# Stores of the second half of w_out's operands: from SyncE's queue to GpSimd's

## The chip, the cores and the metric

The kernel runs on one core of a Trainium2 chip. The metric is the device time of one execution in microseconds (us). The core has five engines that run their own instruction streams and meet at semaphores: TensorE (PE), VectorE (DVE), ScalarE (ACT), GpSimd (POOL) and SyncE (SP). SP computes nothing here: it issues DMAs. ACT and POOL can issue DMAs too. Each of the three has its own instruction stream, in which a DMA that has to wait holds back whatever stands behind it.

## The reference

One layer of a streaming encoder over 4096 prompt rows and 32 sample rows of width 1024, all in float32:

```
h = rmsnorm(x);  proj = h @ w_in                    # 1024 x 5120
u, v, z_a, xb, z_b = split(proj)
a = u * chunk_mlp(layernorm(v)) * silu(z_a)         # mixing of positions, 8 heads
b = pool_mix(x_ext) * silu(z_b)                     # trailing means 2, 4, 8, 16, linear map by group
y = x + concat(a, b) @ w_out                        # w_out: 2048 x 1024
y_out = rmsnorm(y)
```

## The kernel before

Every large product is one step of a seven-product scheme on 2x2 blocks: each operand is turned into seven combinations (q = 0 to 6), each combination is split into a high part (rounded to TensorE's float32r) and a low part (the rest), and TensorE multiplies high by high, high by low and low by high. The program goes through these stages:

- a first stage makes v and the combinations of x, which are stored in DRAM (`xops`);
- four stages (`Set`), one per quarter of the rows, make a and b and store them transposed in DRAM (`abT`);
- two stages (`OutPair`, z = 0 and z = 1) multiply by the upper and the lower 1024 rows of w_out. The stage z = 0 adds its products to x and stores the sum in DRAM (`part`); z = 1 loads it, adds its own products, normalises and stores the output.

In an out stage the operands of w_out lie in seven big tiles (`slot`), one for each q, and pairs of 128 rows of a or b go by. A pair has seven steps (q = 0 to 6) of 12 matmuls. A step's matmuls end in a PSUM bank, and DVE adds the bank to the tile `y` (L724). ACT makes the high part of a pair's operand (L677), DVE the low part (L81), five steps ahead of the multiplication.

The operands of w_out are made beside the stage before the one that uses them and go through DRAM (`wops`). The object `OutWeights(z, k)` does it in seven steps for each of four k: ACT casts the high part (L119), DVE subtracts it to get the low part (L81), then the two, which lie side by side in one tile of 512 KB, are stored (L652). For z = 0 that tile is a `wop`; for z = 1 it is one of the six tiles `raw`. The 28 steps of z = 1 run beside the pairs of stage z = 0, one in every three of their steps. The six `raw` tiles also take the loads of the pairs' rows (L669, from `abT`), rows of w_in (L1209) and the sources of later steps. A tile that was stored from can be written again only when its store has landed. In stage z = 1, each `slot` is loaded from `wops` (L634) when PE has used up its old contents.

SP's stream holds, in this stretch, the loads of w_out (L646), of `abT` (L669), of x into `y` (L703), of w_in (L1209), of a small stack (L1207), and the 28 stores of the operands (L652). A load L703 into a `y` tile waits until the store of its old contents (L735, `part<-y`, in POOL's stream) has landed. There are six `y` tiles, two for each pair. A scheduler sets the order within each engine's stream from the order in the code and its own estimates.

Of the kernel before, what the change touches and what calls it, by code (L numbers as in the profile page):

```python
# [8 lines left out]
F32 = mybir.dt.float32  # L9
# [27 lines left out]
def stream_step(ctx: ExitStack, tc, x_prompt, x_sample, state_pool, norm_g, w_in, ln_v_g, ln_v_b,  # L37
# [9 lines left out]
    nc = tc.nc  # L47
# [63 lines left out]
    def weight_ops(a1, a2, b1, b2, sums, dst, in_order=False):  # L111


        keep = {}
        less = lambda o, x, y: nc.vector.tensor_tensor(o, x, y, ALU.subtract)  # L115

        def split(q, src):
            hi, lo, *then = dst(q)
            pair = nc.scalar.copy(hi, src), lo_part(lo, src, hi)  # L119
            if q == 0 and in_order:  # L120
                for ins in pair:
                    tc.keep_in_program_order(ins)
            if behind:
                behind.pop()
                tc.keep_in_program_order(pair[0])
            for step in then:
                step()

        def third():
            keep[1], keep[2] = sums(), sums()  # L130
            less(keep[1], b1, a1)
            less(keep[2], b2, keep[1])
            split(2, keep[2])

        def fourth():
            less(b1, b2, b1)
            split(3, b1)

        def last():
            less(a2, a2, keep[2])  # L140
            split(6, a2)

        return [lambda: split(0, a1), lambda: split(1, a2), third, fourth, lambda: split(4, keep[1]),
                lambda: split(5, b2), last]
# [66 lines left out]
    with ExitStack() as ph:  # L211
# [142 lines left out]
        class Past:  # L354


            def load(self):
                self.st = half(), half()
                for z in range(2):
                    nc.gpsimd.memset(self.st[z][:HALO], 0.0)  # L360
                    nc.sync.dma_start(self.st[z][1:HALO], state_pool[0, 0, :, z * 512:(z + 1) * 512])
# [259 lines left out]
    def raw_tile(dt=F32):  # L621
        return raw_p.tile([P, D], dt, tag="raw", name="raw")

    def weight_tile():
        return op_p.tile([P, 2, 4, P], F32R, tag="wop", name="wop")
# [10 lines left out]
    class OutWeights:  # L636
# [5 lines left out]
        def load(self):  # L642
            v = []
            for i in range(2):
                raw = self.tile()
                nc.sync.dma_start(raw, w_out_v[8 * self.z + 4 * i + self.k])  # L646
                v.append(raw.rearrange("p (s c e) -> p s c e", s=2, e=P))

            def dst(q):
                t = weight_tile() if self.z == 0 else raw_tile(F32R).rearrange("p (h k t) -> p h k t", h=2, k=4)  # L650
                out = wops[self.z, q, :, self.k, :]
                store = lambda: nc.sync.dma_start(out, t.rearrange("p h k t -> p (h k t)").bitcast(F32))  # L652
                return t[:, 0], t[:, 1], store

            self.prep = weight_ops(v[0][:, 0], v[1][:, 0], v[0][:, 1], v[1][:, 1], sum_tile, dst)
# [530 lines left out]
    with ExitStack() as ph:  # L1186
# [56 lines left out]
        for n in range(n_sets, len(groups)):  # L1243
# [6 lines left out]
            for m, (s, q) in enumerate(order):  # L1250
# [4 lines left out]
                k = n - n_sets - 4  # L1255
# [48 lines left out]
```

## Time and profile before

| | |
|---|---|
| time, median of 3 runs | 2347.77 us (2347.44 to 2348.26) |
| time of the profiled execution | 2347.65 us |
| its span | 2345.9 us |
| PE busy | 2328.8 us (99%) |
| DVE busy | 1790.2 us (76%) |
| ACT busy | 896.4 us (38%) |
| POOL busy | 215.1 us (9%) |
| TensorE clock granted | full, 0.999 over the span |
| share of DMA engines in q1 (SP's transfers and others of that kind) | 45.9% |
| share in q0 (transfers that POOL issues) | 8.3% |

The time is 1.75 us more than the span (2347.65 against 2345.9); what lies around the span isn't in the profile. The span is measured from the first to the last instruction. A wait in the profile names the engine and line that ended it; idle time matters only on the engine that sets the end.

### The profile page before, as it was taken

Reading aid. Unit: us, or ns where it says so; the run is one execution under the profiler, and the core shown is the slowest. Engines: PE = TensorE matmul, PEld = TensorE weight load, DVE = VectorE, ACT = ScalarE, POOL = GpSimd, SP = SyncE. Lnnn points to the kernel's source line nnn. Section 1 sums busy time; section 2 is a strip of 40 time slices with the busy share of each in tenths; the row PEclk is TensorE's granted clock in tenths of the full one; section 3 lists DMA queues with packets and bytes.
Section 4 is the critical chain, followed back from the end, with each engine's and each line's share of the span. In section 5 each row is a group of like instructions: output and inputs, shape, how many; then the busy total and the mean of one; then the engine's idle time right before and its main releaser. Section 6 shows DMA issues by size and latency. Waiting matters only on the chain.

```text
span 2345.9 us, 32604 instructions
## 1 busy us (share of the span) xinstructions
PE 2328.8 (99%) x11936; PEld 1981.3 (84%) x11936; DVE 1790.2 (76%) x3318; ACT 896.4 (38%) x1603; POOL 215.1 (9%) x398
## 2 busy tenths in 40 slices
PE   8999999999999999999999999999999999999998
PEld 7878888888888888888888899999987878888877
DVE  7877786866787767877668876668777778688887
ACT  6545544433433333433334333334322333233333
POOL 1010000100021000111000110102200000000000
PEclk9999999999999999999999999999999999999999
DMA  8879977432448334483334472335587776955542
GB/s 309 316 241 279 275 255 245 142 104 89 149 144 296 99 100 134 135 300 122 108 108 148 177 262 87 101 100 164 223 294 265 252 257 232 360 171 169 159 137 90
DMA packets 325145, 445.69 MB, mean 190 GB/s; under 512 B 19324, under 2 KB 248444, under 8 KB 322296
## 3 DMA queue, kind: packets, MB, share of 16 engines
q1 hardware_dynamic: 273384, 355.05, 45.9%
q0 software_dynamic: 22288, 73.48, 8.3%
q10 hardware_dynamic: 29312, 15.08, 2.4%
q8 instruction: 94, 1.54, 0.3%
q14 instruction: 67, 0.55, 0.1%
HBM read 273.88 MB, written 169.66 MB: 189 GB/s over the span
## 4 chain that ended last, share of the span: by engine, by line
PE 95%; DMA 2%; DVE 2%; issue 0%; ACT 0%; SPq 0%; ACTq 0%; DVEq 0%
PE acc L193 66%; PE acc L712 8%; PE acc L713 8%; PE acc L714 8%; PE sp L998 2%; PE tr L473 1%; DMA wops<-raw 1%; DMA vt<-in_w_in_dram 1%; PE acc L261 0%; DMA op<-in_w_in_dram 0%; PE more L844 0%; PE more L843 0%; DVE wop L81 0%; DVE y L724 0%; PE acc L202 0%
## 5 line engine op out<-in xcount | busy, mean ns | idle before, releaser
L193 PE MATMUL acc<-slot,wop 128*128 128x512 f32 (+1 forms) x6720 | 1260.9, 348 | 1.0 <-DVE wop L81 1.0
L193 PEld LDWEIGHTS acc<-slot,wop 128*128 128x128 f32 x6720 | 1081.1, 188 | 156.5 <-DVE wop L81 1.4
L81 DVE TENSOR_TENSOR wop<-raw,wop 128x512 fp32r<-128x512 f32 (+1 forms) x510 | 353.4, 695 | 133.0 <-ACT wop L119 121.7
L119 ACT CAST wop<-raw 128x512 fp32r<-128x512 f32 x340 | 210.5, 622 | 384.4 <-PE acc L193 266.9
L712 PE MATMUL acc<-slot,wop 128*128 128x512 f32 x892 | 347.2, 389 | 1.5 <-DVE y L724 1.5
L713 PE MATMUL acc<-slot,wop 128*128 128x512 f32 x892 | 347.1, 389 | 0.0
L714 PE MATMUL acc<-slot,wop 128*128 128x512 f32 x892 | 347.0, 389 | 0.0
L193 PE MATMUL acc<-slot,op 128*128 128x512 f32 x1344 | 323.8, 395 | 0.3 <-ACT vt L167 0.2
L193 PEld LDWEIGHTS acc<-slot,op 128*128 128x128 f32 x1344 | 247.6, 188 | 51.9 <-ACT vt L167 0.7
L165 DVE TENSOR_TENSOR t<-acc,t 128x512 f32<-128x512 f32 (+1 forms) x320 | 186.7, 584 | 120.0 <-ACT t L174 65.5
L724 DVE TENSOR_TENSOR y<-acc,y 128x512 f32<-128x512 f32 x235 | 159.3, 687 | 72.6 <-PE acc L714 72.2
L712 PEld LDWEIGHTS acc<-slot,wop 128*128 128x128 f32 x892 | 167.4, 188 | 37.8 <-ACT wop L677 2.3
L714 PEld LDWEIGHTS acc<-slot,wop 128*128 128x128 f32 x892 | 167.4, 188 | 34.8
L713 PEld LDWEIGHTS acc<-slot,wop 128*128 128x128 f32 x892 | 167.4, 188 | 34.7
L677 ACT CAST wop<-raw 128x512 fp32r<-128x512 f32 x160 | 98.7, 622 | 175.2 <-PE acc L714 164.9
L81 DVE TENSOR_TENSOR wop<-sum,wop 128x512 fp32r<-128x512 f32 x200 | 136.9, 685 | 25.7 <-ACT wop L119 24.9
L1017 POOL DMA_DIRECT2D abT<-t x128 | 69.2, 541 | 843.2 <-DVE t L1029 622.7
L119 ACT CAST wop<-sum 128x512 fp32r<-128x512 f32 x136 | 84.5, 622 | 96.9 <-PE acc L193 72.0
L1040 DVE TENSOR_TENSOR t<-t 128x527 f32<-128x527 f32 (+3 forms) x160 | 111.1, 698 | 0.6
L677 ACT CAST wop<-sum 128x512 fp32r<-128x512 f32 x64 | 39.7, 622 | 119.5 <-PE acc L714 96.3
L174 ACT COPY t<-acc 128x512 f32<-128x512 f32 (+1 forms) x80 | 40.2, 504 | 107.1 <-PE acc L193 105.4
L115 DVE TENSOR_TENSOR sum<-raw 128x512 f32<-128x512 f32 x68 | 46.8, 688 | 44.7 <-DMA raw<-in_w_in_dram 44.1
(236 smaller groups left out, 1955.0 us busy)
## 6 DMA issues: line engine op xcount, KB each, us to landing
raw<-in_w_in_dram SPq DMA_DIRECT2D x102, 512.0 KB, 4.3
xops<-op SPq DMA_DIRECT2D x72, 512.0 KB, 6.1
abT<-t POOLq DMA_DIRECT2D x128, 256.0 KB, 3.8
raw<-abT SPq DMA_DIRECT2D x64, 512.0 KB, 5.0
slot<-xops SPq DMA_DIRECT2D x30, 1024.0 KB, 9.6
slot<-wops SPq DMA_DIRECT2D x14, 2048.0 KB, 9.7
xt<-in_x_prompt_dram SPq DMA_DIRECT2D x32, 512.0 KB, 5.0
raw<-v_all SPq DMA_DIRECT2D x32, 512.0 KB, 3.3
```

What stands on the lines that cost most here:

```text
L81: return nc.vector.tensor_tensor(out, src, hi.bitcast(F32), ALU.subtract)
L119: pair = nc.scalar.copy(hi, src), lo_part(lo, src, hi)
L165: add = lambda o, x, y: nc.vector.tensor_tensor(o, x, y, ALU.add)
L193: mm(acc, stationary(s, k), moving(m, k), start=fresh and n == 0, stop=n == len(terms) - 1, skip_group_check=True)
L677: nc.scalar.copy(t[:, 0], src)
L712: mm(acc, x[:, 0, k, :], w[:, k, 0, c], start=fresh and k == 0, stop=False, skip_group_check=True)
L713: mm(acc, x[:, 0, k, :], w[:, k, 1, c], start=False, stop=False, skip_group_check=True)
L714: mm(acc, x[:, 1, k, :], w[:, k, 0, c], start=False, stop=k == 3, skip_group_check=True)
L724: nc.vector.tensor_tensor(y, self.acc[bank], y, ALU.add)
L998: mm(sp[:, a, :], self.v[:, 4 * hf + a, :], WT[:, h, :], start=True, stop=True)
L1017: nc.gpsimd.dma_start(abT[row, :, t0:t0 + HALF], t[:, :HALF])
L1040: tt(nxt[:, lo:HALO + m], s[:, lo:HALO + m], s[:, lo - step:HALO + m - step], ALU.add)
```

## The change

The store of an operand of w_out is issued by GpSimd when z is 1, and by SyncE, as it was, when z is 0. Tiles, sources, destinations and arithmetic stay the same.

```diff
             def dst(q):
                 t = weight_tile() if self.z == 0 else raw_tile(F32R).rearrange("p (h k t) -> p h k t", h=2, k=4)
                 out = wops[self.z, q, :, self.k, :]
-                store = lambda: nc.sync.dma_start(out, t.rearrange("p h k t -> p (h k t)").bitcast(F32))
+                queue = nc.gpsimd if self.z else nc.sync
+                store = lambda: queue.dma_start(out, t.rearrange("p h k t -> p (h k t)").bitcast(F32))
                 return t[:, 0], t[:, 1], store
```

One line is added, so line numbers above 652 rise by one: the store is L653 after the change, the load of `y` L704, the store of `part` L736.

The 28 stores leave SP's stream and enter POOL's. PE's stream keeps its order, and on DVE and ACT a few neighbours change places. In SP's stream of before, in the stretch from about 1900 to 1932 us, three stores of the operands (`raw_17286`, `raw_17347`, `raw_17414`) stand between loads:

```order
L669 DMA raw_17279<-abT_66 128x4x256
L669 DMA raw_17281<-abT_66 128x4x256
L703 DMA y_17521<-in_x_prompt_dram 128x1024
L703 DMA y_17522<-in_x_prompt_dram 128x1024
L652 DMA wops_70<-raw_17286 128x1024
L1209 DMA raw_17378<-in_w_in_dram 128x1024
L646 DMA spare_17277<-in_w_out_dram 128x1024
L652 DMA wops_70<-raw_17347 128x1024
L1207 DMA st_17376<-stk_74 128x128
L652 DMA wops_70<-raw_17414 128x1024
L669 DMA raw_17437<-abT_66 128x4x256
L703 DMA y_17690<-in_x_prompt_dram 128x1024
```

In SP's stream of the changed kernel, at the same place:

```order
L670 DMA raw_17279<-abT_66 128x4x256
L670 DMA raw_17281<-abT_66 128x4x256
L704 DMA y_17521<-in_x_prompt_dram 128x1024
L704 DMA y_17522<-in_x_prompt_dram 128x1024
L1210 DMA raw_17378<-in_w_in_dram 128x1024
L646 DMA spare_17277<-in_w_out_dram 128x1024
L1208 DMA st_17376<-stk_74 128x128
L670 DMA raw_17437<-abT_66 128x4x256
L670 DMA raw_17439<-abT_66 128x4x256
L704 DMA y_17690<-in_x_prompt_dram 128x1024
```

The stores are gone, and the second load from `abT` (`raw_17439`) now stands ahead of the load of `y_17690`. POOL's stream of before holds only the stores of `part` there:

```order
L735 DMA part_71<-y_17048 128x1024
L735 DMA part_71<-y_17049 128x1024
L735 DMA part_71<-y_17206 128x1024
L735 DMA part_71<-y_17207 128x1024
L735 DMA part_71<-y_17368 128x1024
```

POOL's stream of the changed kernel, at the same place:

```order
L736 DMA part_71<-y_17048 128x1024
L736 DMA part_71<-y_17049 128x1024
L653 DMA wops_70<-raw_17286 128x1024
L653 DMA wops_70<-raw_17347 128x1024
L653 DMA wops_70<-raw_17414 128x1024
L736 DMA part_71<-y_17206 128x1024
L736 DMA part_71<-y_17207 128x1024
L653 DMA wops_70<-raw_17483 128x1024
```

The three stores stand behind the stores of one pair's `part` and ahead of the next pair's.

## Rows read from the trace of the kernel before

**Rows 1.** The page: busy time of each engine, and the chain that ended last
```profile
PE 2328.8 (99%) x11936; PEld 1981.3 (84%) x11936; DVE 1790.2 (76%) x3318; ACT 896.4 (38%) x1603; POOL 215.1 (9%) x398
PE 95%; DMA 2%; DVE 2%; issue 0%; ACT 0%; SPq 0%; ACTq 0%; DVEq 0%
```

**Rows 2.** All waits of PE: line, releaser, us in total, times, longest
```profile
PE tr L402 <- DMA vt<-in_w_in_dram: 1.9, 1, 1.9
PE acc L712 <- DVE y L724: 1.5, 2, 1.1
```

**Rows 3.** PE's timeline round its two waits: start, us, engine, line, instruction
```profile
1871.97 0.39 PE L714 MATMUL acc<-slot,wop 128*128 128x512 f32 x1
1872.72 0.47 PE L712 MATMUL acc<-slot,wop 128*128 128x512 f32 x1 [0.37 <-DVE y L724]
...
1932.52 0.39 PE L714 MATMUL acc<-slot,wop 128*128 128x512 f32 x1
1934.05 0.47 PE L712 MATMUL acc<-slot,wop 128*128 128x512 f32 x1 [1.15 <-DVE y L724]
```

**Rows 4.** The chain of waits, 1845 to 1875 us: start, us, what
```profile
1851.04 0.68 DVE raw L81
...
1852.41 6.61 DMA wops<-raw
...
1859.78 0.70 DVE raw L81
1860.50 0.33 SPq L646
...
1860.87 5.45 DMA wops<-raw
```

**Rows 5.** The chain of waits, 1910 to 1936 us
```profile
1913.68 0.32 SPq L703
...
1914.09 6.23 DMA wops<-raw
...
1921.08 0.70 DVE raw L81
...
1922.17 5.47 DMA wops<-raw
```

**Rows 6.** DVE's timeline at 1911 us: the low part of the second chain's first tile
```profile
1911.58 0.68 DVE L81 TENSOR_TENSOR raw<-spare,raw 128x512 fp32r<-128x512 f32 x1
```

**Rows 7.** SP's waits, then ACT's, in 1740 to 2000 us
```profile
SPq L703 <- DMA part<-y: 73.7, 19, 11.5
...
ACT raw L119 <- DMA wops<-raw: 32.6, 9, 6.4
```

**Rows 8.** The stores on SP (L652), 1740 to 2000 us: count, ns, landing
```profile
L652 SPq DMA_DIRECT2D wops<-raw x28: 319/324/1298, 1745.5 to 1991.4; - x28
...
DMA to landing us min/median/max: 2.6/3.9/9.2
```

**Rows 9.** The stores of part on POOL (L735), 1700 to 2000 us
```profile
L735 POOL DMA_DIRECT2D part<-y x24: 531/531/557, 1759.8 to 1990.5; - x24
...
DMA to landing us min/median/max: 2.8/5.0/6.8
```

**Rows 10.** POOL's timeline at 1865 us: a store of part
```profile
1865.09 0.53 POOL L735 DMA_DIRECT2D part<-y  x1 [17.51 <-DVE y L724]
```

**Rows 11.** SP's timeline: loads of y and third store, then the slots
```profile
1867.80 0.32 SPq L652 DMA_DIRECT2D wops<-raw  x1
...
1991.44 0.32 SPq L652 DMA_DIRECT2D wops<-raw  x1
...
1996.06 5.77 SPq L634 DMA_DIRECT2D slot<-wops  x2
...
2006.94 19.36 SPq L634 DMA_DIRECT2D slot<-wops  x5
```

**Rows 12.** Busy time: us, PE, PEld, DVE, ACT, POOL, clock, DMA, GB/s
```profile
1740.00:2000.00 260.00, 258.48 (x1138) 209.98 (x1138) 194.49 (x303) 80.86 (x131) 14.97 (x28) 1.00 0.76 256
```

## The prediction

> **What bounds the kernel now.** I read the page first: PE is busy for 2328.8 of 2345.9 us and carries 95% of the chain that ended last [rows 1]. No queue can win more than the 17.1 us that PE isn't busy. Next, all of PE's waits over the whole span [rows 2]: the reader is to see that in the stage the change touches PE waits only twice, 1.5 us in all, for DVE's addition of a bank to `y`. The longest other wait, 1.9 us, is for a load ahead of the first products, which no moved store reaches; the rest are 1.4 us or less, all in earlier stages. So the ceiling of this change is small and can be read exactly. In this stage a matmul takes PE 258.48 / 1138 = 0.23 us [rows 12]; round the two waits the starts are once 0.75 us apart (1871.97 to 1872.72) and once 1.53 (1932.52 to 1934.05) [rows 3]. That is 0.52 + 1.30 = 1.82 us lost, a little more than the idle 0.37 + 1.15 that the view names, since the pipeline also has to fill again.
>
> Then I ask what made DVE late, in the chain of waits behind each of them [rows 4, 5]. The reader is to see the same pattern twice: a store `wops<-raw` of 6.2 to 6.6 us, then ACT's cast into that tile and DVE's subtraction, then a second store of 5.5 us. ACT's cast of the next operand waits until the store ahead of it has landed (32.6 us in 9 waits in this stretch, the longest 6.4 [rows 7]). ACT works in order, so the pairs' own casts (L677) and DVE's work behind them stand still too. PE lives on its lead of five steps and runs dry at the end of the second landing.
>
> **The change part by part.** *The issue of a store.* In the first chain the low part is ready at 1851.04 + 0.68 = 1851.72 and SP issues at 1852.41: 0.69 late. The second store is ready at 1859.78 + 0.70 = 1860.48 and goes out at 1860.87, behind the load L646: 0.39 late [rows 4]. In the second chain the first store is ready at 1911.58 + 0.68 = 1912.26 [rows 6] and goes out at 1914.09: 1.83 late, right behind a load of `y` (L703, 1913.68). The second is ready at 1921.08 + 0.70 = 1921.78 and goes at 1922.17: 0.39 late [rows 5]. SP stood at L703 because the old `y` had not yet landed in `part`; over the stretch that cost SP 73.7 us in 19 waits, the longest 11.5 [rows 7]. On POOL neither load stands ahead: the POOL order shows three stores in a row between two pairs' `part`. I take 0.05 us of lateness for each, as SP shows when nothing stands ahead (1860.48 to 1860.50, for the load L646). That removes 0.69 + 0.39 - 0.10 = 0.98 us from the first chain and 1.83 + 0.39 - 0.10 = 2.12 from the second.
>
> *The landing.* On SP the 28 stores land 2.6 to 9.2 us after issue, median 3.9 [rows 8]; the four in the chains took 6.61, 5.45, 6.23 and 5.47, since each goes out right behind another load. The trace shows no `wops` store on POOL. The nearest row is POOL's store of `part`, the same 512 KB from SBUF to DRAM in the same stretch: 2.8 to 6.8 us, median 5.0 [rows 9]. I take 5.0, and keep 2.8 and 6.8 as ends.
>
> *How much the chain may take.* A chain's length is its two latenesses and two landings. The first is 0.69 + 6.61 + 0.39 + 5.45 = 13.14 us and PE loses 0.52, so PE loses nothing at 12.62. The second is 1.83 + 6.23 + 0.39 + 5.47 = 13.92 and loses 1.30: again 12.62. That both give the same number is why I trust it. On POOL: 0.10 + 5.0 + 5.0 = 10.1 us, 2.5 below the limit, so both waits go. With the landings exactly as they were on SP the chains are 0.10 + 12.06 = 12.16 and 0.10 + 11.70 = 11.80, and both waits still go, by 0.46 and 0.82. With 6.8 each it is 13.7, PE loses 1.08 twice, 2.16 instead of 1.82: 0.3 slower than before. With 2.8 the waits just go.
>
> *What POOL pays.* 28 issues of 0.531 us [rows 9] are 14.9 us more on an engine that is busy 14.97 of 260 [rows 12]. The price is order: a store of `part` that now stands behind the third store of a chain is late. In the first chain it was issued at 1865.09 [rows 10]; the third `wops` store went out at 1867.80 [rows 11]; so `part` goes at 1868.3, 3.2 us late. Waiting for it is SP's load of x into that `y`, which is for the third pair after (six tiles, two a pair; a pair is 7 steps of 12 matmuls at 0.23, some 19 us). Two pairs of cover hide 3.2 us; without cover it would be 3.2 us of PE in each of the two places.
>
> *What SP gains and loses.* 28 issues of 0.32 us go [rows 8], hidden anyway. Loads issue earlier where a store was ahead of them. The second load from `abT` now stands ahead of two loads of `y`; it waits for the landing of the chain's third store, as it did. Its reader comes several steps later, and the `y` behind it have the cover above. I cost both at nothing.
>
> *The change of stage.* The last store was issued at 1991.44 and the seven slots are loaded from 1996.06 on [rows 11], each when PE lets go of the old one. On POOL that store stands behind `part` of a finished pair and the small store L1239. A few us late would still meet slots of which the last are loaded some 30 us later. Nothing is taken for it.
>
> *A rule that speaks against it.* POOL's issue of `part` takes 531 to 557 ns [rows 9] while DVE is busy 194.49 of 260 us [rows 12], so the row shows no issue held up by a DVE instruction. The Trainium skill's page "SBUF — State Buffer" (Summary: rules for kernel authors) advises against a GpSimd DMA under DVE work: its descriptors are written by GpSimd, which a DVE instruction in one of the faster modes locks out, so one should issue from ACT or SP. By the rule this would cost what the last rival below costs; by the rows, nothing.
>
> **The sum.** 2347.65 (own time of the profiled execution) - 1.82 = 2345.83. The median of the runs shown is 2347.77, 0.12 above it, so the median should come to 2345.95; I say 2346.0.
>
> **The rivals.**
> - *The landing eats it.* POOL's stores share the DMA engines (0.76 busy in this stretch [rows 12]) with the same loads, and land in 6.4 to 6.8 us. For it: 6.8 has been seen on POOL. Against: the median of 5.0. The waits stay as they were or half: 2346.7 to 2348.1, about 2347.7.
> - *Slower: a store on POOL lands in 9.2 us*, as the longest on SP did [rows 8], because loads that SP no longer holds back all run beside it. Place: the cast L119 in the same two chains. The chain is then 0.10 + 18.4 = 18.5, PE loses 18.5 - 12.62 = 5.9 twice, 11.8 instead of 1.82: 2357.7. It decides from landings of 6.26 us on the mean (half of 12.52), and makes the kernel slower than before from 6.7. Against: no POOL store of 512 KB in the stretch was above 6.8.
> - *POOL's issue held by DVE.* If each store waits for one DVE subtraction of 0.68 us [rows 6], the first chain is 12.16 + 1.36 = 13.52 and loses 0.90, the second 11.80 + 1.36 = 13.16 and loses 0.54; 1.44 instead of 1.82: 2347.4 on the scale of the median.
>
> **How the numbers follow.** Both waits go: 0.66. The landing eats it: 0.21. Held by DVE: 0.05. Slower: 0.08, of which more than half is less than the full price. A measurement of this kernel can tell 0.2%, 4.7 us, from no change. The first three cases lie within it. Faster by more would need PE time that no row shows: 0.01. Slower by more is the worst part of the slower case: 0.03. So 0.96 for no change. The range: below, 2345.95 less the spread of the runs shown (0.4) is 2345.5, taken as 2345.3; above, 2348.4, which takes in the case of landings of 6.8 and the spread, and leaves out most of the slower case.
>
> **What would show it.** Right: in the changed kernel PE has no wait on L724's additions in the out stages, the matmuls follow 0.23 us apart all through, ACT's waits for `wops<-raw` fall below 32.6 us, POOL's L653 lands at about 5 us, and SP still stands at L704 but nothing of PE hangs on it. Wrong: waits of PE on L724 of over 1.5 us, L653 landing above 6.7 us, or PE waiting for a `y` or `abT` load that was not late before.

## The result and the profile after

The changed kernel took 2354.54 us, median of 9 runs (2353.38 to 2358.07); the kernel before took 2348.05 beside it (9 runs, 2346.07 to 2349.99). The ratio is 1.0029, 95% interval [1.0021, 1.0038]: slower by 6.5 us, more than the 0.2% that the prediction took as the least change that can be told. The prediction of 2346.0 us with a range up to 2348.4 and 0.03 for slower was wrong. The profiled execution took 2353.82 us with a span of 2352.0, 6.1 more than before.

The page after, to be set against [rows 1]:

```profile
PE 2332.2 (99%) x11936; PEld 1984.0 (84%) x11936; DVE 1789.9 (76%) x3318; ACT 895.6 (38%) x1603; POOL 230.3 (10%) x426
PE 92%; issue 3%; DMA 2%; DVE 2%; ACT 0%; POOL 0%; SPq 0%; POOLq 0%; DVEq 0%; ACTq 0%
```

PE is still 99% busy. It does the same 11936 matmuls, yet its busy time rose by 3.4 us: some matmuls ran slower. PE's two largest items of waiting over the span (line, releaser, us in total, times, longest), against [rows 2]:

```profile
PE acc L713 <- DVE y L725: 6.0, 3, 3.8
PE tr L402 <- DMA vt<-in_w_in_dram: 1.6, 2, 0.9
```

The two waits of 1.5 us for the addition into `y` became three of 6.0 us. PE's timeline shows where (start, us, engine, line, instruction, idle before it):

```profile
1792.05 0.39 PE L715 MATMUL acc<-slot,wop 128*128 128x512 f32 x1
1793.72 0.47 PE L713 MATMUL acc<-slot,wop 128*128 128x512 f32 x1 [1.28 <-DVE y L725]
...
1799.06 0.39 PE L715 MATMUL acc<-slot,wop 128*128 128x512 f32 x1
1803.22 0.76 PE L713 MATMUL acc<-slot,wop 128*128 128x512 f32 x1 [3.77 <-DVE y L725]
1803.78 0.63 PE L714 MATMUL acc<-slot,wop 128*128 128x512 f32 x1
1804.20 0.63 PE L715 MATMUL acc<-slot,wop 128*128 128x512 f32 x1
...
1808.47 0.56 PE L713 MATMUL acc<-slot,wop 128*128 128x512 f32 x1
1808.87 0.39 PE L714 MATMUL acc<-slot,wop 128*128 128x512 f32 x1
...
1879.21 0.39 PE L715 MATMUL acc<-slot,wop 128*128 128x512 f32 x1
1880.51 0.47 PE L713 MATMUL acc<-slot,wop 128*128 128x512 f32 x1 [0.91 <-DVE y L725]
```

Less the pace of 0.23, the start-to-start gaps cost 1.44, 3.93 and 1.07 us. Behind the second, 13 matmuls take 5.65 us (1803.22 to 1808.87) instead of 13 x 0.23 = 2.99, another 2.66. That is 9.1 us, against 1.82 before: 7.3 more. The stage starts about 1.0 us earlier than before (the first slot load at 1671.63 instead of 1672.63), which leaves 6.3, beside 6.1 in the spans. The wait that stood at 1933 before is gone; the one near 1872 has a counterpart at 1879. The big one, near 1799, and the one at 1792 have no counterpart in [rows 2].

What released it is on DVE and ACT. DVE's timeline of the changed kernel, then ACT's:

```profile
1795.41 0.69 DVE L692 TENSOR_TENSOR raw<-raw,sum 128x512 f32<-128x512 f32 x1
1801.78 0.69 DVE L81 TENSOR_TENSOR raw<-spare,raw 128x512 fp32r<-128x512 f32 x1 [5.67 <-ACT raw L119]
1802.39 0.68 DVE L725 TENSOR_TENSOR y<-acc,y 128x512 f32<-128x512 f32 x1
1802.99 0.68 DVE L81 TENSOR_TENSOR wop<-sum,wop 128x512 fp32r<-128x512 f32 x1
```
```profile
1792.16 1.13 ACT L678 CAST wop<-raw 128x512 fp32r<-128x512 f32 x2
1801.13 0.62 ACT L119 CAST raw<-spare 128x512 fp32r<-128x512 f32 x1 [7.83 <-issue]
1801.65 0.61 ACT L678 CAST wop<-sum 128x512 fp32r<-128x512 f32 x1
```

DVE stands still for 5.67 us at the subtraction of an operand of w_out, and the addition that empties PE's bank stands right behind it. The subtraction waits for ACT's cast, and the cast (which the view gives as "issue") starts 0.07 us after the seventh store has landed: that store is issued at 1793.27 and lands at 1801.06. The same place on DVE in the kernel before:

```profile
1796.18 0.69 DVE L724 TENSOR_TENSOR y<-acc,y 128x512 f32<-128x512 f32 x1 [0.65 <-PE acc L714]
1796.83 0.69 DVE L81 TENSOR_TENSOR wop<-sum,wop 128x512 fp32r<-128x512 f32 x1
1800.76 0.69 DVE L81 TENSOR_TENSOR raw<-spare,raw 128x512 fp32r<-128x512 f32 x1 [3.24 <-ACT raw L119]
```

There the same subtraction also waits (3.24 us), but the addition is ahead of it and costs PE nothing. The order of the two programs on DVE, before and after, says why:

```
2471 L724 TENSOR_TENSOR y_16271<-acc_16282,y_16271 128x512
2472 L81 TENSOR_TENSOR wop_16364<-sum_16361,wop_16364 128x512
2473 L81 TENSOR_TENSOR raw_16468<-spare_16331,raw_16468 128x512

2471 L81 TENSOR_TENSOR raw_16468<-spare_16331,raw_16468 128x512
2472 L725 TENSOR_TENSOR y_16271<-acc_16282,y_16271 128x512
2473 L81 TENSOR_TENSOR wop_16364<-sum_16361,wop_16364 128x512
```

`raw_16468` is the eighth operand of the 28 (k = 1, q = 0). The change touched no instruction of DVE, but the scheduler moved this subtraction two places up. On ACT its cast moved one place up, ahead of the cast of `wop_16364`, and nothing else moved there. On DVE eight more rows change places, between 1874 and 2023 in the changed kernel. Two of these are the same swap, a subtraction of an operand of w_out that moves ahead of one addition, once in each of the two chains of [rows 4, 5].

The stores themselves, by line in this stretch (the landing is from issue to completion), against [rows 8]:

```profile
L653 POOL DMA_DIRECT2D wops<-raw x28: 531/531/557, 1744.4 to 1998.7; - x28
...
  ACT raw L119: 37.8, 9
...
DMA to landing us min/median/max: 2.9/5.5/7.8
```

The landing is 5.5 us in the median instead of 3.9, with a maximum of 7.8 instead of 9.2, and ACT's waits for it rose from 32.6 to 37.8 us; the 7.83 us that the view gives as "issue" come on top. The store that matters here, the seventh, took 7.79 us (1793.27 to 1801.06), and 6.45 before (1793.58 to 1800.03).

### The profile page after: what moved, and what is told of

Read it like the earlier page. It is cut to its first block, busy times and chain, and to the rows that moved or that the text cites. A ratio compares the mean times of both kernels' runs of the same rounds, so it can differ in the third digit from the quotient of the medians.

```text
span 2352.0 us, 32627 instructions
## 1 busy us (share of the span) xinstructions
PE 2332.2 (99%) x11936; PEld 1984.0 (84%) x11936; DVE 1789.9 (76%) x3318; ACT 895.6 (38%) x1603; POOL 230.3 (10%) x426
## 4 chain that ended last, share of the span: by engine, by line
PE 92%; issue 3%; DMA 2%; DVE 2%; ACT 0%; POOL 0%; SPq 0%; POOLq 0%; DVEq 0%; ACTq 0%
PE acc L193 66%; PE acc L713 7%; PE acc L715 7%; PE acc L714 7%; PE sp L999 2%; PE tr L473 1%; DMA vt<-in_w_in_dram 1%; DMA wops<-raw 1%; DMA op<-in_w_in_dram 0%; PE more L845 0%; DVE y L725 0%; PE more L844 0%; DVE wop L81 0%; PE acc L202 0%; PE acc L201 0%
```

## Experiments

Every time stands beside runs of the kernel before on the same chip (2347.73 to 2347.76 us, 27 or 33 runs); ratios carry their 95% intervals, and as they are not taken from the two medians they can differ from these by a few 0.0001. In the quotations theory A is that the place of the eighth operand in the order makes the loss; it began as its place on ACT. The other letters are its rivals, as each quotation says. The edits are shown shortened. Where an order is changed, it is by an edge that makes one instruction stand behind another on the same engine (some runs name the function `behind_cast`):

```diff
+    def place_behind(ins, other):
+        edge = mybir.DependencyInfo(mybir.DependencyClass.NoSync, mybir.DependencyReason.DATA)
+        tc.add_manual_dep(ins.ins, other.ins.name, edge, reason="order")
```

`pair` is the cast and the subtraction of an operand, `casts` the casts into `wop` and `adds` the additions into `y` so far.

**e1_pin: the changed kernel, the cast of the eighth operand back behind the cast of `wop_16364` on ACT.**

```diff
+            if pin and q == 0:            # z = 1, k = 1
+                place_behind(pair[0], casts[-6])
```

> The changed kernel, with one edge added that puts ScalarE's cast of the eighth operand (the first of k = 1, raw<-spare) back behind the cast of the pair's operand (wop<-sum) that stood ahead of it before the change. The 28 stores stay on GpSimd. Theory A (the order on ScalarE is the cause: the changed kernel put that cast one place earlier, where it waits 7.8 us for a store to land, and a cast that TensorE needs stands behind it): the wait of 3.77 us at 1799 us and the matmuls at half rate behind it go; what is left of waits on the addition to y is 1.3 + 0.9 us, perhaps one more below 1.5; time 2348 to 2349.5, at most 1.5 above before. Theory B (the stores' longer landing on GpSimd's queue is the cause, the place of the cast is not): the store in front still lands at 1801 us, TensorE still waits 3 to 4 us there, time 2353 to 2355.

Measured: 2347.88 us, 1.0001 [0.9992, 1.0009]. The whole loss is gone, with all 28 stores still on POOL. The seventh store landed even later than in the changed kernel (1801.17, after 7.98 us), the cast waited 3.93 us for it, and PE had a single wait in the stage, of 1.1 us at 1792. But the edge also put DVE's order back, so the run doesn't tell ACT's place from DVE's.

**e2_swap: the kernel before, with that cast and subtraction earlier.** The operand was traced two steps earlier, and its cast placed behind `casts[-5]`.

> The kernel before, all stores on SyncE, with the cast of the eighth operand put one place earlier on ScalarE, ahead of the pair's cast (wop<-sum), as the changed kernel has it. Theory A: that cast waits for the store in front until about 1800 us, the pair's cast stands behind it, TensorE waits 2.5 to 4 us near 1798 us and may run slow behind it; with the two waits of before (1.5 us idle) the time is 2351 to 2354, 3 to 6 above before. Theory B: the landing on SyncE is as before, so nothing moves: 2347.5 to 2348.5.

Measured: 2347.81 us, 0.9999 [0.9991, 1.0008]. For theory A as it stood the run is inconclusive: traced earlier, the operand no longer depends on the seventh store, probably by another `raw` tile, and its cast at 1792.54 had no landing to wait for. On DVE its subtraction did stand ahead of the addition (1793.27 against 1794.73), so the order without a landing to wait for cost nothing.

**e3_pool_prep_sw: the changed kernel, with cast and subtraction of the 28 operands on GpSimd.**

```diff
-            pair = nc.scalar.copy(hi, src), lo_part(lo, src, hi)
+            pair = (nc.gpsimd.tensor_copy(hi, src),          # z = 1 only
+                    nc.gpsimd.tensor_tensor(lo, src, hi.bitcast(F32), ALU.subtract))
```

> The changed kernel, with the cast and the subtraction of w_out's second-half operands done by GpSimd instead of ScalarE and VectorE, so that only GpSimd ever waits for one of these stores to land. Theory A and theory B both put all of TensorE's waits in this stage down to ScalarE standing at a landing, so both expect them to go: no wait on the addition to y in this stage, span 2343 to 2345, time 2345.5 to 2347, 1 to 2.5 below before. Rival C (VectorE is the late one by itself, or GpSimd's arithmetic slows VectorE): waits on the addition to y remain, VectorE's subtraction takes more than 0.69 us beside GpSimd's work, time 2348 or more.

Measured: 2348.49 us, 0.9999 [0.999, 1.0008]. With the operands off ACT and DVE, GpSimd alone waits for the landings, and PE has two short waits left in the stage (1.0 us for an operand, 0.7 for an addition). The time of 2345.5 to 2347 that theories A and B gave was missed, and the signs named for rival C came: GpSimd's arithmetic has a price. GpSimd and DVE by line in this stretch (busy us, mean ns of one, idle before):

```profile
L121 POOL TENSOR_TENSOR raw<-spare,raw 128x512 fp32r<-128x512 f32 x20 | 31.9, 1593 | 1.7
L120 POOL CAST raw<-spare 128x512 fp32r<-128x512 f32 x20 | 16.3, 817 | 57.6 <-DMA wops<-raw 52.1 <-DVE wop L81 3.3 <-DMA spare<-in_w_out_dram 1.9
```
```profile
L81 DVE TENSOR_TENSOR wop<-sum,wop 128x512 fp32r<-128x512 f32 x26 | 21.1, 810 | 0.1
L115 DVE TENSOR_TENSOR spare<-spare 128x512 f32<-128x512 f32 x4 | 6.0, 1501 | 0.0
```

DVE's subtractions of the form that took 0.69 us before (mean of 26) take 0.81 in the mean, and the four additions `spare<-spare`, 0.69 before, take 1.50.

**e5_k0_sync: the changed kernel, the seven stores of k = 0 back on SP.**

```diff
-                queue = nc.gpsimd if self.z else nc.sync
+                queue = nc.gpsimd if self.z and self.k else nc.sync
```

> The changed kernel, with the first seven of the 28 stores (k = 0) back on SyncE and 21 on GpSimd; ScalarE's order at the eighth operand is then that of before. Theories A and B both put about 7 of the 9 us that TensorE loses into the stretch of these seven: the waits at 1792 and 1799 us and the half rate go, one wait of about 0.9 us near 1879 us stays, the one of 1.15 us of before near 1933 us is gone as in the changed kernel; time 2347 to 2348.5, as before within 1 us. If the loss were one of GpSimd's queue in general, three quarters of it would stay: 2352 to 2353.5.

Measured: 2346.68 us, 0.9994 [0.9985, 1.0002]. The waits at 1792 and 1799 are gone; 0.25 us at 1871 and 1.13 at 1932 stay, where 0.9 near 1879 and nothing near 1933 was expected. The scheduler also put the addition back ahead of the subtraction, so this too fits order and landing alike.

**e6_swap_only: the kernel before, with ACT's order alone as in the changed kernel.** The edge is `place_behind(casts[-6], pair[0])`, and the operand keeps its tile.

> The kernel before, all stores on SyncE and SyncE's order untouched, with one edge that puts the pair's cast (wop<-sum) behind ScalarE's cast of the eighth operand. Unlike in the swap tried first, the eighth operand keeps its tile, so its cast waits for the seventh store to land, as in the changed kernel. Theory A (place and landing wait together): the seventh store lands near 1800 us, the pair's cast starts near 1800.6 instead of 1796.2, TensorE waits some 3 us on the addition to y near 1799 us, perhaps with a dozen matmuls at half rate behind it; time 2350.5 to 2353.5, 3 to 6 above before. Theory B (only the longer landing on GpSimd's queue matters): 2347.3 to 2348.5, as before.

Measured: 2348.02 us, 1.0002 [0.9994, 1.0011]. ACT stood 5.24 us at the cast, and PE lost nothing near 1799: on DVE the addition (1795.15) still stood ahead of the subtraction (1798.95). Two DVE rows moved with the edge: the subtraction went one place up, ahead of that of `wop_16364` but still behind the addition, and `raw<-raw` (L687) two places down. Theory A in its first form, the place on ACT, fell here. What was left was the place on DVE.

**e7_act_queue: the stores in ACT's queue instead of GpSimd's** (`queue = nc.scalar if self.z else nc.sync`).

> The 28 stores issued in ScalarE's queue. Read for the landing of the stores, which on SyncE took 3.9 us in the median and on GpSimd 5.5. Theory D (on any queue other than SyncE's the store runs beside SyncE's loads and shares the DMA engines with them): median 5 us or more. Theory E (it is GpSimd's own making of the transfers): median about 4, as on SyncE. ScalarE now also waits for VectorE before each store, so TensorE's waits may be other ones and the time up to 10 us more; the time tells nothing of D and E.

Measured: 2350.39 us, 1.0015 [1.0006, 1.0024], slower than before by 2.7 us. Its PE waits, stores and windows (us; PE, PEld, DVE, ACT, POOL busy; granted clock; DMA share; GB/s):

```profile
PE acc L713 <- DVE y L725: 3.7, 1, 3.7
```
```profile
DMA to landing us min/median/max: 2.6/5.3/7.6
```
```profile
1802.00:1806.00 4.00, 4.00 (x12) 3.15 (x11) 2.60 (x5) 0.00 (x0) 0.00 (x0) 0.57 0.53 167
```

The landing is 5.3 us here too. So the longer landing is not of GpSimd's making alone: it came with both queues in which the stores no longer stand between SP's loads. And the same wait of PE is back; in this kernel too the scheduler put the subtraction of `raw_16468` ahead of the addition.

**e8_pin_all and e9_before_pin_all: every one of the 28 casts behind `casts[-4]`, in the changed kernel and in the kernel before.**

> The changed kernel, each of the 28 casts of w_out's second half put behind the pairs' cast that stands four steps back in the code, so that none runs ahead and stands at a landing before casts that TensorE needs soon. Theory A: TensorE has no wait of over 0.5 us on the addition to y in this stage, time 2345.5 to 2347, 1 to 2 below before. If the lead of the pairs' casts is too short whatever the order: waits of 1 us or more stay, 2347.5 or more.

> The same 28 edges with all stores on SyncE, as before the change. Theory A: the two waits of before (1.5 us idle) go here too or shrink below 0.5 us, time 2345.5 to 2347, and it differs from the same edges on GpSimd's queue by less than 1 us: with the order right, the queue doesn't matter. Theory B: it is 1 us or more faster than with GpSimd's queue, whose landings are longer.

Measured: 2347.68 us, 1.0001 [0.9992, 1.001], and 2349.6 us, 1.0009 [1.0, 1.0018]. With one rule for the order the stores on GpSimd cost nothing against before, but the rule doesn't take all waits away: 0.54 and 1.04 us remain in the first, 0.46, 0.59 and 0.89 in the second, where less than 0.5 was expected. The two kernels also differ by 1.9 us, GpSimd's queue being the faster, where theory A expected less than 1 and theory B the opposite sign; the reason stays open.

**e10_dve_swap: the kernel before, all stores on SP, and on DVE the addition behind the subtraction.** Nothing on PE, ACT, POOL or SP changes its place. On DVE the low part of `wop_16364` stays ahead of both, and one more row moves: `raw<-raw` (L687) goes two places down.

```diff
+            if pin and q == 0:            # z = 1, k = 1
+                place_behind(adds[-8], pair[1])
```

> Kernel before (all stores on SyncE), with one order changed: on VectorE the addition into y that empties a bank stands behind the subtraction of the eighth operand (k = 1, q = 0), as in the changed kernel; ScalarE's order stays as before. Theory A' (place on VectorE, not queue): the cast waits for the seventh store until about 1800, the subtraction ends about 1801.4, the addition about 1802.1, so TensorE loses about 3.4 us there and perhaps another 2.5 us by the half clock behind it; 2351 to 2353.6 us. Rival (the longer landings of the stores on GpSimd are needed): as before, 2347.7 us within 0.7, no wait of TensorE over 1.2 us near 1800.

Measured: 2352.66 us, 1.0023 [1.0014, 1.0032]: slower by 4.9 us without any store moved. DVE's timeline, PE's, and two windows:

```profile
1799.29 0.69 DVE L81 TENSOR_TENSOR raw<-spare,raw 128x512 fp32r<-128x512 f32 x1 [1.81 <-ACT raw L119]
1799.90 0.68 DVE L732 TENSOR_TENSOR y<-acc,y 128x512 f32<-128x512 f32 x1
```
```profile
1798.43 0.39 PE L722 MATMUL acc<-slot,wop 128*128 128x512 f32 x1
1800.73 0.47 PE L720 MATMUL acc<-slot,wop 128*128 128x512 f32 x1 [1.91 <-DVE y L732]
...
1802.03 0.63 PE L722 MATMUL acc<-slot,wop 128*128 128x512 f32 x1
```
```profile
1798.00:1802.00 4.00, 2.09 (x9) 1.41 (x8) 2.71 (x5) 1.14 (x2) 0.00 (x0) 0.98 0.90 370
1803.00:1806.00 3.00, 3.00 (x10) 2.38 (x9) 0.74 (x2) 0.62 (x1) 0.00 (x0) 0.62 0.80 231
```

The same pattern stands at the same place. The wait is 1.91 us in the profiled execution instead of the 3.4 expected, because the seventh store landed at 1798.56 instead of about 1800, and eight matmuls follow 0.43 apart. Waits of 0.97 us at 1753, 0.82 at 1877 and 0.36 at 1937 stand beside it; the first has no counterpart in the kernel before.

**e11_dve_pin: the changed kernel, all stores on GpSimd, with DVE's order put back.** The edge is `place_behind(pair[1], adds[-8])`; ACT's order stays as the scheduler made it. Of the streams of all five engines, this subtraction on DVE is the only row that has another place than in the changed kernel.

> Changed kernel (stores on GpSimd), with one order put back on VectorE: the addition into y and the subtraction of one wop stand again ahead of the subtraction of the eighth operand; ScalarE's order stays as in the changed kernel. Theory A': the wait of 3.8 us and the half clock behind it go (6.5 us), waits of about 1.3 and 0.9 us from the longer landings stay, 2347.5 to 2349.5 us. Rival (ScalarE's order or the landings alone set it): 2353 to 2355 us, a wait of TensorE of over 3 us near 1800.

Measured: 2349.05 us, 1.0006 [0.9997, 1.0015]. DVE's timeline and PE's waits:

```profile
1796.70 0.69 DVE L733 TENSOR_TENSOR y<-acc,y 128x512 f32<-128x512 f32 x1 [0.67 <-PE acc L723]
1802.51 0.69 DVE L81 TENSOR_TENSOR wop<-sum,wop 128x512 fp32r<-128x512 f32 x1 [5.12 <-ACT wop L686]
1803.12 0.68 DVE L81 TENSOR_TENSOR raw<-spare,raw 128x512 fp32r<-128x512 f32 x1
```
```profile
PE acc L721 <- DVE y L733: 2.3, 2, 1.3
```

The seventh store lands at 1801.27, as late as in the changed kernel, ACT stands 7.72 us at its cast, and PE has no wait at 1799. Two waits for the addition are left, 1.06 us at 1806 and 1.27 at 1875, and one of 0.69 for an operand at 1794.

**e12_both_sync: the kernel before, all stores on SP, with both orders of the changed kernel**, on ACT and on DVE (the edges of e6 and e10 together).

> Kernel before (all stores on SyncE), with both orders of the changed kernel at the eighth operand: its cast ahead of the cast of a wop on ScalarE and its subtraction ahead of the addition into y on VectorE. Theory A': as the kernel with VectorE's order alone changed, a wait of TensorE of 3 to 3.8 us near 1800, 2351 to 2353.6 us. Rival (GpSimd's queue is needed): as before, 2347.7 us within 0.7.

Measured: 2351.92 us, 1.0016 [1.0007, 1.0025]: slower by 4.2 us. On DVE the three rows stand as in the changed kernel. PE waits 2.50 us near 1798 and 1.5 near 1934 in the profiled execution, which was the shortest of the eleven (2349.51). Adding ACT's order to DVE's makes it no worse.

**after_again: the changed kernel once more**, beside e10 to e12.

> The changed kernel once more, as the measure for the run with VectorE's order put back: 2353.5 to 2355 us by every theory.

Measured: 2355.91 us, 1.0034 [1.0022, 1.0047], above the expected range; in its profile PE waits 3.92 us near 1800, as in the first one, and also 1.81 at 1754, where the first has no wait. So on this chip the change costs 8.1 us. Putting one subtraction on DVE back behind two neighbours gives 6.9 of them back (2355.91 to 2349.05; 2354.5 to 2357.39 against 2347.25 to 2351.13), and the 1.3 that stay can't be told from no change. No kernel here was measurably faster than the kernel before; e5, at 0.9994, came nearest.

## Why the prediction was wrong

**The step that failed is one that has no term in the sum.** The prediction took PE's two waits as all there was to gain or lose, priced POOL's and SP's order, and cost the neighbours that change places on DVE and ACT, told of ahead of it, at nothing without a word. One such pair is the loss: with it the kernel before becomes 4.9 us slower (e10), and without it the changed kernel gets 6.9 us back (e11). An addition into `y` has little cover. In e10 the step's products end by 1796.14, when a cast of ACT that waits for them starts, and the last matmul that PE can do without the bank starts at 1798.43, 2.3 us later. The operands of the same step have five steps. Moving an instruction that waits for a landing ahead of that addition turns ACT's and DVE's idle time, which cost nothing, into PE's.

It could have been priced from the kernel before:

```profile
1798.70 0.39 PE L712 MATMUL acc<-slot,wop 128*128 128x512 f32 x1
...
1933.22 0.69 DVE L724 TENSOR_TENSOR y<-acc,y 128x512 f32<-128x512 f32 x1
```

The addition starts at 1796.18, as PE releases it, and the bank is due some 2.5 us later, at 1798.70. The subtraction starts at 1800.76. With the addition behind it, that starts at 1801.37, 0.61 later. Where PE waited for an addition before, it went on 0.83 after its start (1933.22 to 1934.05 [rows 3]), which is 1802.2 here: 3.5 us lost. The changed kernel lost 3.93 there.

The loss needs both the place and a landing: e2 has the place on DVE without the landing, e11 the landing (at 1801.27) without the place, and neither has the loss. A landing on SP is enough; the later one on GpSimd probably makes the loss larger. With the stores on SP the seventh lands at 1798.56 (e10) and 1798.37 (e12) in the profiles, and the swap costs 4.9 and 4.2 us; on GpSimd it lands at 1801.06 and the swap costs 6.9. No run moves the landing alone with the swap in place.

The prediction named waits of PE of over 1.5 us on the addition as a sign that it is wrong, and that sign came. The rivals missed the place: the slower one had cast and landing right, but its place was the two chains of [rows 4, 5], not a third place where PE didn't wait before.

**The clock behind the wait had no term either.** The windows of the changed kernel behind the stop:

```profile
1740.00:2000.00 260.00, 254.03 (x1105) 205.70 (x1104) 190.46 (x296) 77.97 (x128) 29.85 (x56) 0.99 0.71 244
1803.00:1809.00 6.00, 5.78 (x14) 4.59 (x15) 3.54 (x7) 0.29 (x1) 0.30 (x1) 0.51 0.54 180
```

The granted clock is 0.51, the lower level of 1.2 GHz, for some 5.6 us after PE stood 3.77 us. That is 2.66 us of the 7.3. Over the whole run the mean granted clock is 0.997 or 0.998 in all five executions of after_again, and 0.999 in all eleven of e11.

**The two waits, landing and lateness.** "Both waits go" was half right: one went. The terms were mis-sized. The landing was taken as 5.0 us; in the chains it was 6.82 and 5.51, and 5.63 and 5.55. The lateness was taken as 0.05, from a load on SP; it was 0.52 and 0.30 in the first chain: the low part is ready at 1858.27 + 0.69 = 1858.96 and POOL issues at 1859.48, then 1867.05 + 0.69 = 1867.74 and 1868.04.

```profile
1859.48 0.53 POOL L653 DMA_DIRECT2D wops<-raw  x1 [4.63 <-issue]
1868.04 0.53 POOL L653 DMA_DIRECT2D wops<-raw  x1 [8.03 <-DVE raw L81]
```

All 28 stores on POOL start 0.29 to 0.53 us after the low part, where the shortest on SP was 0.03; why POOL starts later stays open.

The first chain is so 0.52 + 6.82 + 0.30 + 5.51 = 13.15 us, and PE loses 1.07 behind it; the second is 0.52 + 5.63 + 0.30 + 5.55 = 12.00, and PE loses nothing. The form of the step held, but the limit is 13.15 - 1.07 = 12.08 here and no longer 12.62. That comes from the same kind of swap. DVE's timeline from the chain's last subtraction to the addition that PE waits for, before and after:

```profile
1867.07 0.69 DVE L81 TENSOR_TENSOR raw<-spare,raw 128x512 fp32r<-128x512 f32 x1 [2.28 <-ACT raw L119]
...
1871.89 0.69 DVE L724 TENSOR_TENSOR y<-acc,y 128x512 f32<-128x512 f32 x1
```
```profile
1874.27 0.69 DVE L81 TENSOR_TENSOR raw<-spare,raw 128x512 fp32r<-128x512 f32 x1 [2.80 <-ACT raw L119]
1874.88 0.68 DVE L725 TENSOR_TENSOR y<-acc,y 128x512 f32<-128x512 f32 x1
...
1879.68 0.68 DVE L725 TENSOR_TENSOR y<-acc,y 128x512 f32<-128x512 f32 x1
```

An addition that stood ahead of that subtraction now stands behind it, so the way is 5.41 us instead of 4.82. The limit goes with the order in every run read for it: wherever PE loses over 0.3 us behind a chain, chain less loss is 12.62 to 12.64 in e6, e10 and e12, which keep the old order there, and 12.06 to 12.08 in the changed kernel, after_again, e5 and e11, which have the new one. In all of these the chain's stores are on SP with the old order and on GpSimd with the new, so that it is the order and not the queue rests on DVE's 0.59 us.

The wait of 1.28 us at 1792 comes from a longer landing: the store ahead of the sixth cast lands after 6.43 us instead of 3.61. In e11 the waits at 1794 and 1875 stand at the places of the changed kernel's first and third. The one at 1806 is, by the timelines, the price of ACT's order, which e11 leaves: DVE waits 5.12 us for the cast of `wop_16364`, and an addition stands behind it; e1, where that cast is back in its place, has no such wait.

**What held.** POOL's issues took 531 to 557 ns, so none was held by DVE while it ran, as the rows of `part` said. POOL's later stores of `part`, SP's new order and the change of stage cost PE no wait. In e1, where order alone was mended, the time was that of before, with a single wait of 1.1 us left in the stage.

## What to carry to other kernels

When a scheduler orders the streams, a store that changes its queue also changes the order on engines that it never touches: compare those orders row by row, and price every pair of neighbours that changes places. Ask of each which one waits for a transfer and which one the bounding engine needs soonest; a wait that costs nothing today does so only because of what stands ahead of it. Here the instruction that empties a PSUM bank had a cover of one step, whatever lead the operands had.

## What was not expected of the hardware

- **The landing was longer on both other queues.** The 28 stores took 3.9 us in the median on SP [rows 8], 5.5 on GpSimd and 5.3 on ACT. On SP a store stands between loads; on either other queue it can run beside them, which would explain it; no run tests that by itself. Stores on GpSimd also landed in 2.9 to 3.2 us (issued at 1790.09, 1802.77, 1875.26 and 1935.19), so the queue itself takes little: the shortest landing is 2.9 on GpSimd and 2.6 on SP and ACT.
- **PE's clock fell to its lower level after some stops, and not by their length alone.** It fell after 3.77 us (the changed kernel), 3.73 (e7) and 1.91 (e10, where the slow matmuls begin 1.3 us after PE went on); the means over the windows shown are 0.51, 0.57 and 0.62. After 2.50 us, in the profiled execution of e12, it stayed at 1.00:

```profile
1797.64 0.39 PE L724 MATMUL acc<-slot,wop 128*128 128x512 f32 x1
1800.53 0.47 PE L722 MATMUL acc<-slot,wop 128*128 128x512 f32 x1 [2.50 <-DVE y L734]
1800.84 0.40 PE L723 MATMUL acc<-slot,wop 128*128 128x512 f32 x1
```
```profile
1803.00:1806.00 3.00, 3.00 (x15) 2.49 (x14) 2.92 (x5) 0.62 (x1) 0.00 (x0) 1.00 0.89 265
```

  Five of e12's other ten executions have a mean clock of 0.998 over the run instead of its 0.999, so the same stop may end either way. What decides it stays open. In e10 the stop of 1.91 us cost PE 3.7 us: 2.07 between the starts, and 1.6 by the slow matmuls behind it.
- **Arithmetic on GpSimd slowed DVE** (0.69 to 0.81 us in the mean, and 1.50 for one form, in e3). Single instructions took up to 1.79 us, all of them while GpSimd was subtracting; the additions out of PSUM kept 0.69. GpSimd's issuing of stores didn't show in DVE's durations: the additions took 0.69 us in both kernels.
